# Ordering a bank's matrix products by width, and an earlier transpose of attention keys, in a ten-stage float32 network on Trainium2

## The chip, the cores and the metric

The kernel is one program on one core of a Trainium2 chip. The metric is the device time in microseconds of one execution; lower is better. Before the change it is 2365.12 us, the median of three runs. Engines are named as in the profile: PE (TensorE, matrix products), PEld (TensorE's loads of the stationary operand), DVE (VectorE), ACT (ScalarE), POOL (GpSimd) and SP (SyncE, which issues the DMAs).

## What is computed

Two blocks of two layers each, on 256 tokens of width 1024, in float32. The first has mixers (spatial gating with latent attention, and retention) and gated feed-forwards; the second puts in each layer a feed-forward, a hybrid of three attention branches, and a feed-forward. Cut to the two parts that the change touches:

```python
def swiglu(h, w_gate, w_up, w_down):
    return (jax.nn.silu(h @ w_gate) * (h @ w_up)) @ w_down

def swa_sink_attention(q, k, v, sinks):
    ...
    s = jnp.einsum('bnqhgd,bnkhd->bnhgqk', q, kb).astype(jnp.float32) * (D_C ** -0.5)
    s = s - slopes[:, :, None, None] * jnp.abs(dist).astype(jnp.float32)
    ...
    p = jax.nn.softmax(jnp.concatenate([s, sink], axis=-1), axis=-1)[..., :-1].astype(v.dtype)
    o = jnp.einsum('bnhgqk,bnkhd->bnqhgd', p, vb)

def hybrid_mixer(x, w_in, b_in, ...):
    proj = x @ w_in + b_in
    (qa, ka, va, beta_raw, a_raw, za, qb, kb, vb, qc, kc, vc) = jnp.split(proj, split_at, axis=-1)
    o_a = gated_deltanet(qa, ka, va, beta_raw, a_raw, za, ...)
    o_b = chunk_relpos_attention(qb, kb, vb, rel_bias)
    o_c = swa_sink_attention(qc, kc, vc, sinks)
    gates = jax.nn.sigmoid(x @ w_gate + b_gate).reshape(b, t, N_BRANCH, d)
    merged = (gates[:, :, 0] * (o_a @ w_br_a) + gates[:, :, 1] * (o_b @ w_br_b)
              + gates[:, :, 2] * (o_c @ w_br_c))
    return merged @ w_out
```

## The kernel before

**Stages.** Ten in a row: the even mixer, a feed-forward, the odd mixer, a feed-forward, then for each of two layers a feed-forward (32 column tiles of 128), a hybrid and a feed-forward. The 256 tokens are two blocks of 128. Activations stay in SBUF; the weights, 415.95 MB in all, are streamed once.

**Accuracy and weights.** Each float32 operand is split into a high and a low part of the type fp32r, and a product is three: high by high, high by low, low by high. `prep` (L137) brings a unit of weights, up to 128 x 2048, in two halves: a DMA on SP's queue into `raw` (L148, five buffers), a cast on ACT to `hi` (L149, four buffers) and a subtraction on DVE to `lo` (L150, four buffers). Up to four units are prepared ahead; `pump` and `more` issue them as units are used up.

**A bank of products.** `x_tile` (L350) makes 128 output columns for all 256 tokens in one PSUM bank of 512 float32 columns. The weights are the stationary operand. `x2[:, k]` holds the activations' high part beside their low part, 512 columns, and `xT[0][:, k]` the high part alone, 256 columns. For each of the eight slices k of the width, the weights' high part `u[0]` multiplies all 512 columns into the whole bank, and the weights' low part `u[1]` multiplies the 256 columns into its second half. A pair below is one such product of 512 and one of 256. `fold` (L360) then adds the halves: a copy on ACT (L263) and an addition on DVE (L241). `mm` (L230 in the trace) issues a product, `tr` (L238) a transpose, which is a product with the identity `ident`.

`apair` (L332) uses two banks for a unit (projections of the even mixer, and the hybrid's convolution inputs, queries, keys and gates); the feed-forward's `chunk` (L614) uses four, two of the gate and two of the up weights, and after it come the down products `emit_down` (L641), 512 columns each with activations as the stationary operand. PSUM's eight banks are four called acc and four called work. In a feed-forward acc holds the down projection's sums and the chunks use work; in a hybrid layer `x_tile` takes acc, and the attention tasks take work.

**A hybrid layer.** `bulk` (L1100) is a generator that issues the projections one after the other and announces events: "kvc" after the opening, in which keys and values of the grouped attention, the deltanet's beta and decay inputs and its gate za are projected; "qkv" after six `apair` of the convolution's inputs; "qc" after two for the grouped attention's queries; "qkvb" after those of the other attention. After each piece of `bulk` the tasks are stepped once: `tasks_cb` (the grouped attention `task_c`, L1203, then `task_b`) and `task_a` (the deltanet). So tasks fill in between projections. In `task_c` the keys of the two token blocks are transposed into a work bank, copied to `kcT` and multiplied by the queries; the alibi table is added (L253), `softmax` (L678) follows with exponentials on ACT, `p_T` (L702) transposes the weights p, ACT copies them out of PSUM, and PE multiplies them by the values. `task_a` transposes the deltanet's keys, values and queries to tokens, squares them on ACT, sums on DVE (L1323), takes the reciprocal root on POOL (L274) and multiplies on DVE.

**Order.** Each engine works off its own list in order. The framework's scheduler makes the lists from the program's order, the dependences and the buffers, so an edit in one place can move instructions of another task in a list.

Of the kernel before, what the change touches and what calls it, by code (L numbers as in the profile page):

```python
# [117 lines left out]
class Net:  # L118
# [231 lines left out]
    def x_tile(self, u, j):  # L350


        ps = self.acc() if self.gacc else self.work()
        c = slice(128 * j, 128 * j + 128)
        for k in range(8):
            self.mm(ps, u[0][:, k, c], self.x2[:, k], k == 0, False)
            self.mm(ps[:, 256:512], u[1][:, k, c], self.xT[0][:, k], False, k == 7)
        return ps

# [709 lines left out]
    def hyb(self, l, nxt):  # L1069
# [4 lines left out]
        events = set()  # L1074
# [8 lines left out]
        kvc = [None] * 2  # L1083
# [117 lines left out]
                    self.pump()  # L1201

        def task_c():  # L1203
            while "qc" not in events:
                yield "wait"
            kcT = self.tile(256)
            ps = self.work()
            for b in range(2):
                self.tr(ps[:, 128 * b:128 * b + 128], kvc[b][:, 0:128])
            self.cp(kcT, ps[:, 0:256])  # L1210
            ali = self.table("alibi", 384)
            yield
            qcT = late["qcT"]
            for b in range(2):
                nk = b + 1
                if b == 0:
                    oT[2] = self.pair(4)
                for half in range(2):
                    pr = slice(64 * half, 64 * half + 64)
                    s = self.tile(4, 128 * nk)  # L1220
                    for j in range(nk):
                        per = 4 // nk
                        bank = self.work()
                        for i in range(per):
                            h = per * j + i
                            c = slice(128 * nk * i, 128 * nk * i + 128 * nk)
                            self.mm(bank[:, c], qcT[pr, h, 128 * b:128 * b + 128], kcT[pr, 0:128 * nk])
                        for i in range(per):
                            h = per * j + i
                            c = slice(128 * nk * i, 128 * nk * i + 128 * nk)  # L1230
                            self.stt(s[:, h], ali[:, 128 * b:128 * b + 128 * nk], -float(2.0 ** -(4 * half + h + 1)), bank[:, c], ALU.mult, ALU.add)
                    p = self.softmax(s, 4, 128 * nk, 1.0, sinks[:, 4 * half:4 * half + 4])
                    yield
                    yield
                    pT = self.p_T(p, 4, nk)
                    yield
                    po = self.work()
                    pq = pT.rearrange("p (k e) n q -> p k e n q", e=2)
                    for e in range(2):
                        for kb in range(nk):  # L1240
                            self.mm(po[64 * e:64 * e + 64, 0:256].rearrange("p (k q) -> p k q", k=2), kvc[kb][:, 128 + 64 * half:192 + 64 * half],
                                    pq[:, :, e, kb], kb == 0, kb == nk - 1)
                    d = [t[:, 2 * half:2 * half + 2, 128 * b:128 * b + 128] for t in oT[2]]
                    self.split(d[0], d[1], po[:, 0:256].rearrange("p (k q) -> p k q", k=2))
                    yield
            events.add("o2")
# [266 lines left out]
        def tasks_cb():  # L1513
            yield from task_c()
            yield from task_b()
# [158 lines left out]
```

## Time and profile before

| | before |
|---|---|
| median of three runs | 2365.12 us (2364.11 to 2366.49) |
| the profiled execution | 2366.65 us, its span 2364.6 us |
| mean granted TensorE clock | 0.993 |
| PE busy | 2328.1 us, 98% of the span |
| DVE, ACT, POOL busy | 64%, 52%, 4% |
| chain that ended last | PE 96%, DVE 1%, POOL 1% |
| DMA | 419.14 MB, mean 177 GB/s |

Busy times are sums over instructions of one engine, from one profiled execution; the span leaves out some two microseconds of the time. A matmul's own duration in a row overlaps its neighbours', since matmuls are pipelined: the distance from one start to the next tells what one takes from the engine. The chain is followed backwards from the last instruction; an engine with nearly all of it sets the end. In the rows, a word in brackets is the idle time before an instruction and what ended it.

### The profile page before, as it was taken

What the parts mean: (1) busy time and instruction counts of PE and PEld (TensorE: products, weight loads), DVE (VectorE), ACT (ScalarE), POOL (GpSimd) and SP (SyncE); (2) the same over time, 40 slices, a digit from 0 to 9 for tenths busy, and PEclk for the clock granted to TensorE, in tenths of its full rate; (3) what the DMA queues carried; (4) which work ended last, traced back from release to release, by engine and by line L of the source; (5) the groups of instructions that cost most, each with busy time, mean ns of one, the idle gap of its engine ahead of it and who ended that gap; (6) DMA issues with size and microseconds to landing.
All of it is one profiled execution on the core that took longest, in us unless ns stands there. A gap on an engine that the chain in (4) does not pass through costs nothing.

```text
span 2364.6 us, 32735 instructions
## 1 busy us (share of the span) xinstructions
PE 2328.1 (98%) x12670; PEld 1991.7 (84%) x12670; DVE 1523.5 (64%) x2176; ACT 1232.0 (52%) x1942; POOL 94.2 (4%) x149
## 2 busy tenths in 40 slices
PE   8999999999999999999999999999999999999998
PEld 7788888888888888878998888888888789988887
DVE  6665576665565555887666555665567876765555
ACT  6655454454454544754545545455456644554543
POOL 4200000000000000000000000000000000000000
PEclk9999999999999999999999999999999999999999
DMA  7365555555556555543365555565555533565552
GB/s 238 131 210 192 189 193 174 186 186 187 189 181 208 191 186 175 188 143 119 100 205 201 191 187 187 178 210 185 191 173 195 168 103 100 185 209 186 193 185 92
DMA packets 120556, 419.14 MB, mean 177 GB/s; under 512 B 14408, under 2 KB 17224, under 8 KB 120400
## 3 DMA queue, kind: packets, MB, share of 16 engines
q1 hardware_dynamic: 120112, 416.53, 52.8%
q8 instruction: 99, 1.62, 0.3%
q14 instruction: 57, 0.47, 0.1%
q10 hardware_dynamic: 288, 0.52, 0.1%
HBM read 415.95 MB, written 1.05 MB: 176 GB/s over the span
## 4 chain that ended last, share of the span: by engine, by line
PE 96%; DVE 1%; POOL 1%; issue 0%; DMA 0%; ACT 0%; SPq 0%; POOLq 0%; DVEq 0%; ACTq 0%
PE work L230 51%; PE acc L230 42%; PE work L238 3%; DVE lo L150 1%; POOL c L273 0%; DMA raw<-in_w 0%; POOL c L274 0%; DVE s L241 0%; POOL c L853 0%; POOL c L852 0%; DVE s L253 0%; ACT s L260 0%; DVE c L1323 0%; ACT hi L149 0%; PE work L1437 0%
## 5 line engine op out<-in xcount | busy, mean ns | idle before, releaser
L150 DVE TENSOR_TENSOR lo<-raw,hi 128x1024 fp32r<-128x1024 f32 (+3 forms) x772 | 916.8, 1206 | 557.9 <-ACT hi L149 557.2
L149 ACT CAST hi<-raw 128x1024 fp32r<-128x1024 f32 (+3 forms) x772 | 786.0, 1038 | 547.0 <-PE work L230 210.9
L230 PE MATMUL work<-x,hi 128*128 128x512 f32 x2496 | 884.1, 398 | 0.0
L230 PE MATMUL work<-x,lo 128*128 128x256 f32 x2496 | 700.5, 281 | 0.0
L230 PEld LDWEIGHTS work<-x,hi 128*128 128x128 f32 x2496 | 468.9, 188 | 115.0
L230 PE MATMUL acc<-hi,s 128*128 128x512 f32 (+1 forms) x1736 | 555.9, 393 | 0.0
L230 PEld LDWEIGHTS work<-x,lo 128*128 128x128 f32 x2496 | 471.3, 189 | 2.7
L230 PEld LDWEIGHTS acc<-hi,s 128*128 128x128 f32 x1736 | 325.7, 188 | 70.9 <-DVE s L241 1.1
L230 PE MATMUL acc<-lo,s 128*128 128x512 f32 (+1 forms) x868 | 338.2, 390 | 0.0
L230 PE MATMUL acc<-x,hi 128*128 128x512 f32 x800 | 288.6, 403 | 0.0
L230 PE MATMUL acc<-x,lo 128*128 128x256 f32 x800 | 224.9, 281 | 0.0
L230 PE MATMUL work<-hi,x 128*128 128x512 f32 x640 | 205.4, 394 | 0.6 <-DVE x L241 0.5
L241 DVE TENSOR_TENSOR s<-s,s 128x512 f32<-128x512 f32 (+3 forms) x234 | 152.2, 658 | 64.9 <-ACT s L263 54.5
L263 ACT COPY s<-work 128x256 f32<-128x256 f32 (+3 forms) x380 | 151.2, 401 | 80.8 <-PE work L230 57.8
L230 PEld LDWEIGHTS acc<-lo,s 128*128 128x128 f32 x868 | 163.3, 188 | 31.3 <-issue 0.2
L241 DVE TENSOR_TENSOR s<-work,s 128x256 f32<-128x256 f32 (+5 forms) x382 | 165.0, 435 | 27.3 <-ACT s L263 14.3
L230 PEld LDWEIGHTS acc<-x,hi 128*128 128x128 f32 x800 | 151.2, 189 | 34.8
L263 ACT CAST s<-s 128x512 fp32r<-128x512 f32 (+2 forms) x90 | 54.5, 606 | 193.6 <-DVE s L241 193.6
L230 PEld LDWEIGHTS acc<-x,lo 128*128 128x128 f32 x800 | 152.0, 190 | 0.2
L230 PEld LDWEIGHTS work<-hi,x 128*128 128x128 f32 x640 | 119.9, 188 | 26.6 <-DVE x L241 1.8
L230 PE MATMUL work<-s,s 128*128 128x128 f32 (+8 forms) x884 | 125.2, 301 | 10.6 <-ACT s L263 9.9
L230 PEld LDWEIGHTS work<-s,s 128*128 128x128 f32 (+4 forms) x884 | 106.4, 185 | 26.5 <-ACT s L263 11.6
(108 smaller groups left out, 1597.7 us busy)
## 6 DMA issues: line engine op xcount, KB each, us to landing
raw<-in_w SPq DMA_DIRECT2D x748, 512.0 KB, 4.2
s<-in_rows SPq DMA_DIRECT2D x16, 512.0 KB, 6.7
raw<-in_w SPq DMA_DIRECT2D x12, 288.0 KB, 3.2
s<-in_rows SPq DMA_DIRECT2D x9, 256.0 KB, 5.6
raw<-in_w SPq DMA_DIRECT2D x4, 384.0 KB, 7.7
raw<-in_w SPq DMA_DIRECT2D x4, 256.0 KB, 4.4
s<-in_relb SPq DMA_DIRECT2D x2, 512.0 KB, 5.1
raw<-in_w SPq DMA_DIRECT2D x4, 240.0 KB, 2.5
```

Source lines behind the costliest of these rows:

```text
L149: self.nc.scalar.copy(hi[:, a:b], raw)
L150: self.nc.vector.tensor_tensor(out=lo[:, a:b], in0=raw, in1=hi[:, a:b].bitcast(F32), op=ALU.subtract)
L230: self.nc.tensor.matmul(out, lhsT=l, rhs=r, start=start, stop=stop)
L238: self.nc.tensor.transpose(out, src, self.ident)
L241: self.nc.vector.tensor_tensor(out=out, in0=a, in1=b, op=op)
L263: self.nc.scalar.copy(out, a)
```

## The change

Two edits. In `x_tile` the loop over k is split: all eight 512-column products with the weights' high part first, then all eight 256-column ones with the low part. In `task_c` the transposes of the keys and their copy are issued when "kvc" is there and one step has gone by, before the wait for "qc"; the alibi table's load stays behind that wait.

```diff
--- before.py
+++ after.py
@@ -354,6 +354,7 @@
         c = slice(128 * j, 128 * j + 128)
         for k in range(8):
             self.mm(ps, u[0][:, k, c], self.x2[:, k], k == 0, False)
+        for k in range(8):
             self.mm(ps[:, 256:512], u[1][:, k, c], self.xT[0][:, k], False, k == 7)
         return ps
 
@@ -1201,13 +1202,16 @@
                     self.pump()
 
         def task_c():
+            while "kvc" not in events:
+                yield "wait"
+            yield
+            kcT = self.tile(256)
+            ps = self.work()
+            for b in range(2):
+                self.tr(ps[:, 128 * b:128 * b + 128], kvc[b][:, 0:128])
+            self.cp(kcT, ps[:, 0:256])
             while "qc" not in events:
                 yield "wait"
-            kcT = self.tile(256)
-            ps = self.work()
-            for b in range(2):
-                self.tr(ps[:, 128 * b:128 * b + 128], kvc[b][:, 0:128])
-            self.cp(kcT, ps[:, 0:256])
             ali = self.table("alibi", 384)
             yield
             qcT = late["qcT"]
```

On PE in a feed-forward chunk, where `x_1160` is the activations and `hi`, `lo` are the weights' parts, the piece of the difference at the first bank reads:

```order
-L230 MATMUL work<-x_1160,hi 128x512
-L230 MATMUL work<-x_1160,lo 128x256
-L230 MATMUL work<-x_1160,hi 128x512
-L230 MATMUL work<-x_1160,lo 128x256
...
+L230 MATMUL work<-x_1160,hi 128x512 x8
+L230 MATMUL work<-x_1160,lo 128x256 x8
```

Sixteen products of changing width have become a run of eight and a run of eight; the sets are the same.

On PE in the first hybrid layer, around the grouped attention's first half (`acc_9202` a bank of projections, `work_9150` the transposes of the softmax's weights, `work_9183` their product with the values, `work_9188` and `work_9195` transposes of the deltanet's values), before:

```order
L230 MATMUL acc_9202<-x2_8142,lo_8900 128x256
L238 MATMUL work_9150<-ident_75,s2_9060 128x128 x4
L230 MATMUL acc_9202<-x2_8142,hi_8899 128x512
L230 MATMUL acc_9202<-x2_8142,lo_8900 128x256
L230 MATMUL work_9183<-s2_9149,s1_8330 64x256 x2
L238 MATMUL work_9188<-ident_75,s4_8642 128x128 x4
L238 MATMUL work_9195<-ident_75,s4_8642 128x128 x4
```

and now:

```order
L230 MATMUL acc_9202<-x2_8142,hi_8904 128x512 x3
L238 MATMUL work_9150<-ident_75,s2_9060 128x128 x4
L230 MATMUL acc_9202<-x2_8142,hi_8904 128x512 x5
L230 MATMUL acc_9202<-x2_8142,lo_8905 128x256 x8
L230 MATMUL work_9183<-s2_9149,s1_8330 64x256 x2
L238 MATMUL work_9188<-ident_75,s4_8647 128x128 x4
L238 MATMUL work_9195<-ident_75,s4_8647 128x128 x4
```

The transposes of the weights stood behind seven of the bank's eight pairs and stand behind three of its 512s; thirteen of the bank's products, not two, lie between them and the product with the values.

On ACT at the same place (`raw` and `hi_9156`, `hi_9272` weight units, `s2_9046` the scores, `work_9072` and `work_9112` transposed keys of the deltanet), before:

```order
L260 ACTIVATE s4_8960<-s2_9037,colt_80 128x256 x2
L149 CAST hi_9156<-raw_9158 128x1024
L260 ACT_TABLE_LOAD
L260 ACTIVATE s2_9060,c_9061<-s2_9046,c_9056 128x128 x4
L260 ACTIVATE c_9066<-c_9066 128x4
L260 ACTIVATE s2_9077<-work_9072 128x512
L149 CAST hi_9156<-raw_9162 128x1024
L149 CAST hi_9272<-raw_9274 128x1024
L260 ACTIVATE s2_9117<-work_9112 128x512
```

and now:

```order
L260 ACTIVATE s4_8965<-s2_9037,colt_80 128x256 x2
L260 ACT_TABLE_LOAD
L260 ACTIVATE s2_9060,c_9061<-s2_9046,c_9056 128x128 x4
L260 ACTIVATE c_9066<-c_9066 128x4
L260 ACTIVATE s2_9077<-work_9072 128x512
L149 CAST hi_9156<-raw_9158 128x1024
L149 CAST hi_9156<-raw_9162 128x1024
L260 ACTIVATE s2_9117<-work_9112 128x512
L149 CAST hi_9272<-raw_9274 128x1024
```

The first cast of unit 9156 stood ahead of the table load and the exponentials and stands behind the square of `work_9072`; the first cast of unit 9272 stood ahead of the square of `work_9112` and stands behind it.

On DVE there, before:

```order
L1323 TENSOR_REDUCE c_9078<-s2_9077 128x4
L150 TENSOR_TENSOR lo_9157<-raw_9162,hi_9156 128x1024
L241 TENSOR_TENSOR s2_9083<-work_9072,c_9078 128x512
L150 TENSOR_TENSOR lo_9273<-raw_9274,hi_9272 128x1024
L1323 TENSOR_REDUCE c_9118<-s2_9117 128x4
L150 TENSOR_TENSOR lo_9273<-raw_9278,hi_9272 128x1024
L241 TENSOR_TENSOR s2_9123<-work_9112,c_9118 128x512
```

and now:

```order
L1327 TENSOR_REDUCE c_9078<-s2_9077 128x4
L150 TENSOR_TENSOR lo_9157<-raw_9158,hi_9156 128x1024
L241 TENSOR_TENSOR s2_9083<-work_9072,c_9078 128x512
L1327 TENSOR_REDUCE c_9118<-s2_9117 128x4
L150 TENSOR_TENSOR lo_9157<-raw_9162,hi_9156 128x1024
L241 TENSOR_TENSOR s2_9123<-work_9112,c_9118 128x512
```

The reduction of the second square stood behind a subtraction of unit 9273 and follows the multiplication at once.

## Rows read from the trace of the kernel before

**Rows 1.** Page of before, busy time of each engine.
```profile
PE 2328.1 (98%) x12670; PEld 1991.7 (84%) x12670; DVE 1523.5 (64%) x2176; ACT 1232.0 (52%) x1942; POOL 94.2 (4%) x149
```

**Rows 2.** Page, costliest groups: busy us, mean ns of one; idle before.
```profile
L230 PE MATMUL work<-x,hi 128*128 128x512 f32 x2496 | 884.1, 398 | 0.0
...
L230 PEld LDWEIGHTS work<-x,lo 128*128 128x128 f32 x2496 | 471.3, 189 | 2.7
...
L230 PE MATMUL acc<-x,hi 128*128 128x512 f32 x800 | 288.6, 403 | 0.0
```

**Rows 3.** Timeline of PE, 32 pairs of a chunk: start us, us, instruction, [idle before].
```profile
610.79 0.39 PE L230 MATMUL work<-x,hi 128*128 128x512 f32 x1
...
622.08 0.40 PE L230 MATMUL acc<-hi,s 128*128 128x512 f32 x1
```

**Rows 4.** Timeline of PE, 512-column products of the down projection, same view.
```profile
607.84 0.62 PE L230 MATMUL acc<-hi,s 128*128 128x512 f32 x2
...
610.56 0.39 PE L230 MATMUL acc<-hi,s 128*128 128x512 f32 x1
```

**Rows 5.** Timeline of PE, a run of 256 columns and the 512 behind.
```profile
1220.37 0.40 PE L230 MATMUL acc<-s,hi 128*128 128x256 f32 x2
...
1226.49 0.40 PE L230 MATMUL acc<-hi,s 128*128 128x512 f32 x1
...
1228.33 0.62 PE L230 MATMUL acc<-hi,s 128*128 128x512 f32 x2
```

**Rows 6.** Timeline of PE, grouped attention in both hybrid layers.
```profile
1020.93 0.38 PE L238 MATMUL work<-ident,s 128*128 128x128 f32 x2
...
1041.71 0.65 PE L230 MATMUL work<-s,s 128*64 128x256 f32 x4 [3.53 <-ACT s L263]
...
1045.55 1.09 PE L238 MATMUL work<-ident,s 128*128 128x128 f32 x4 [2.14 <-DVE s L241]
...
1882.93 1.09 PE L238 MATMUL work<-ident,s 128*128 128x128 f32 x4 [1.67 <-DVE s L241]
```

**Rows 7.** Windows: us, busy (x) of PE, PEld, DVE, ACT, POOL, PEclk, DMA share, GB/s.
```profile
1042.30:1052.50 10.20, 8.06 (x33) 6.84 (x32) 6.83 (x18) 3.93 (x14) 2.11 (x2) 0.50 0.43 130
76.30:83.10 6.80, 5.88 (x15) 4.64 (x16) 6.20 (x16) 4.74 (x11) 1.21 (x2) 0.50 0.26 80
66.00:73.00 7.00, 6.35 (x42) 5.74 (x43) 4.71 (x10) 4.62 (x8) 5.97 (x10) 1.00 0.22 75
```

**Rows 8.** Timeline of PE, 264 columns right after 512 columns, a hybrid layer's opening.
```profile
954.91 0.28 PE L230 MATMUL acc<-hi,x 128*128 128x264 f32 x1
...
955.88 0.40 PE L230 MATMUL acc<-hi,x 128*128 128x264 f32 x2
```

**Rows 9.** Timeline of ACT ahead of the first hybrid layer's wait.
```profile
1031.82 1.05 ACT L149 CAST hi<-raw 128x1024 fp32r<-128x1024 f32 x1 [0.57 <-ACT s L260]
1032.88 1.28 ACT L260 ACT_TABLE_LOAD   x1
1034.18 0.40 ACT L260 ACTIVATE s<-s,c 128x128 f32<-128x128 f32 x1
```

**Rows 10.** Timeline of DVE, same place.
```profile
1032.57 0.16 DVE L241 TENSOR_TENSOR c<-c 128x4 f32<-128x4 f32 x1
...
1040.59 1.22 DVE L150 TENSOR_TENSOR lo<-raw,hi 128x1024 fp32r<-128x1024 f32 x1
...
1044.71 0.69 DVE L241 TENSOR_TENSOR s<-work,c 128x512 f32<-128x512 f32 x1 [1.18 <-POOL c L274]
```

**Rows 11.** Timeline of SP's queue, same layer.
```profile
1016.99 17.49 SPq L148 DMA_DIRECT2D raw<-in_w  x8
```

**Rows 12.** Timeline of PE, the first stage's two longer waits.
```profile
66.65 0.64 PE L238 MATMUL work<-ident,s 128*96 128x128 f32 x4 [1.18 <-POOL s L854]
...
76.55 1.23 PE L230 MATMUL work<-s,s 128*128 128x128 f32 x4 [2.85 <-ACT s L263]
```

**Rows 13.** Timeline of PEld, weight loads in a run of 256-column products.
```profile
1127.47 0.31 PEld L230 LDWEIGHTS acc<-s,hi 128*128 128x128 f32 x2
...
1128.55 0.31 PEld L230 LDWEIGHTS acc<-s,hi 128*128 128x128 f32 x2
```

More of the change, by code (lines that the diff above doesn't have):

```diff
@@ L1203, in task_c @@
         def task_c():
-            while "qc" not in events:
+            while "kvc" not in events:
                 yield "wait"
+            yield
             kcT = self.tile(256)
@@ L1210, in task_c @@
             self.cp(kcT, ps[:, 0:256])
+            while "qc" not in events:
+                yield "wait"
             ali = self.table("alibi", 384)
```

## The prediction

> **What bounds the kernel now.** I read the busy times first. TensorE (PE) works 2328.1 of 2364.6 us of span [rows 1], so a microsecond counts if TensorE's own instructions get shorter or one of its few waits does. The costliest groups come next: the products that the change reorders are 2496 in work banks and 800 in acc banks, each with a 256-column partner [rows 2]. At eight pairs to a bank that is 3296 / 8 = 412 banks. The durations there (398 and 403 ns) overlap with the neighbours, so no price comes out of them. What a product costs is the distance between starts, from the timeline. In a feed-forward chunk 32 pairs go from 610.79 to 622.08 [rows 3]: 11.29 us, 352.8 ns a pair, **2.822 us a bank**. Products of one width in a row run closer than their shares of that pair: 512 after 512 go from 607.84 to 610.56, 12 in 2.72 us, 226.7 ns each [rows 4], and 256 after 256 take 6.12 us for 51, 120.0 ns each [rows 5]. The sum of the two is 346.7, not 352.8: changing the width costs about 6 ns a pair. Last I looked for TensorE's long waits. Past the opening there are few, and the largest are in the two hybrid layers: 3.53 us before the grouped attention's product of weights and values, then 2.14 us before a transpose in the first layer and 1.67 in the second [rows 6], with the clock at 0.50, the 1.2 GHz level, for 10.2 us from there [rows 7].
>
> **The change, part by part.** *Grouping.* No product is added or removed; a bank keeps its 8 + 8, and the last is still the one that closes it. The width now changes twice a bank instead of sixteen times. What a short run of eight costs has two rows near it. Eight 512-column products right after a run of 256 take 1.84 us, from 1226.49 to 1228.33 [rows 5] (230 ns each: the first ones are slower than the steady 226.7). Eight products of 264 columns right after 512-column ones take 0.97 us, from 954.91 to 955.88 [rows 8]; eight columns less each at 2.4 GHz, the level of a granted clock of 1.00, is 8 x 8 / 2.4 = 27 ns, so 0.943. The new bank is 1.842 + 0.943 = 2.785 us, the gain 0.037 us, times 412 = **15.2 us**. The low end takes the steady 120.0 ns for the 256 (bank 2.802, gain 8.2), the high end the steady 226.7 for the 512 (bank 1.814 + 0.960 = 2.774, gain 20). I take the middle: it comes from the rows nearest to a run of eight behind the other width. A gain of nothing is a rival below.
>
> Against this stands a rule. In these rows a product's price hangs on the one before it (352.8 against 346.7). The Trainium skill, "TensorE: Matmul & The Clock Gate", section "Back-to-back issue gap", gives an isolated gap of columns / 2.4 plus 2.5 ns, in any order: by that a bank is 8 x (215.8 + 109.2) = 2.600 us before and after, and the grouping gains nothing. The trace differs: it shows 2.822.
>
> *What the grouping moves on the other engines.* The low part of a weight unit is wanted eight products later, its high part is free about eight 256-column products (0.96 us) sooner: both ease the casts. As the high buffer is free sooner, its next casts slip ahead of the fold of the bank on ScalarE, and the subtractions ahead of the fold's add on VectorE. Two casts of 1.05 [rows 9], two subtractions of 1.22 [rows 10] and the fold itself are under 6 us; the chunk has four work banks, so a bank is wanted again after three others, 8.4 us. That covers it: nothing. Were the cover gone, the rest would be a TensorE wait at every fourth bank.
>
> *The keys' transposes.* Two transposes, a work bank and a copy go from the point where the queries are ready to the opening of the layer. They are 0.38 us for both as shown [rows 6], about 0.25 in spacing, on TensorE at either place. No engine waits by the generator's wait itself; it decides only where the instructions are issued. The alibi table's DMA (128 x 384, 0.2 MB) falls behind one weight transfer on SP's queue, the first of the eight that were issued from 1016.99 [rows 11]; each of the two is 1.5 to 4 us at the 130 GB/s of a neighbouring stretch [rows 7] (0.2 and 0.5 MB), so it lands by about 1023, and the scores need it shortly ahead of the softmax's last step at 1032.57 [rows 10]. The weight transfer gets ahead of it, which hurts none. Nothing, with several microseconds of cover.
>
> *The hybrid layers' stall.* Both parts reorder the queues here. Before, one cast (1031.82, 1.05 us) stands ahead of the table load (1.28) and so of the softmax's exponentials, which start at 1034.18 [rows 9], though their inputs are there at 1032.57 + 0.16 = 1032.73 [rows 10]. Now the cast comes behind them: 1.4 us. On VectorE a subtraction (1040.59, 1.22 us with its overlap, some 1.1 in spacing) stands ahead of the reduction that the late transpose hangs on by way of POOL and the multiplication at 1044.71 [rows 10]; now the reduction is first: 1.1. The transpose at 1045.55 would be 2.5 us earlier. Of this, the banks between 1020.93 and 1041.71 (some 6 outside the wait) have 0.22 in the grouping's sum already, and 0.25 are the two transposes that only change place: 2.0 a layer, **4.0 us** for both. Ends: 2.5 a layer if nothing is counted twice; a loss of 1.05 if one cast now stands ahead of the copy that the attention waits for. I take the 2.0, since the moves stand in the order. Next late is that copy: between the transposes of the softmax weights and the product that waits, TensorE now has five 512s and eight 256s (2.1 us) instead of one pair (0.35), but they come out of the work ahead, and by estimate some 2.5 us of wait stays there, then 1.2 before the transpose.
>
> **Sum.** 15.2 + 4.0 = 19.2. The profiled execution took 2366.65 us, 1.53 over the median 2365.12; 2366.65 - 19.2 - 1.53 = 2345.9, so **2346.0**.
>
> **The rivals.**
> A, the sum as it stands, clock falling in both layers as before. Its own range is 2340 (20 and 5.0) to 2357 (8.2 and nothing): for it speak [rows 5, 8].
> C, the clock no longer falls in the hybrid layers. The rest of that stretch, 1045.55 to 1052.50, is 6.95 us at the lower level, and 3.5 us come back in each: 2342.4 for one, 2338.9 for both. What the rows say of shorter waits: one wait of 2.85 us, in the first stage, is followed by 0.50, and one of 1.18 by 1.00 [rows 7, 12]. The remaining 2.5 is nearer to 2.85, so C is the less likely.
> B, a product's price does not depend on its neighbours after all, and the 6 ns are lost somewhere else (an operand's place, say): only the 4.0 remain, 2361.1. Against it: the same widths show both prices in one chunk [rows 3, 4]. This is also what the skill's rule above gives; its level disagrees with the trace, so it adds little to the chance.
> D, slower: eight 256-column products in a row leave too little time to load their weights. A load's row is 188 to 189 ns [rows 2]; now a 512-column product stands between two 256s and hides it. If a load had to run by itself, the bank would be 1.84 + 8 x 0.189 = 3.35 us, 0.53 more, 218 in all: 2579. It decides from 122 ns a product ((2.822 - 1.842) / 8). Against it: in a 256-column run nine loads start within 1.08 us, 120 ns apart, though each is shown as 0.19 [rows 13]; those load activations, not weights, the one thing that differs.
>
> **How the numbers follow.** A 0.57, C 0.23, B 0.10, D 0.05, the rest (a partial gain, a new wait that eats some of it) 0.05. The forecast is A's. The range takes A's slow end and C's time for both layers with 2 us for the bank's spread: 2337 to 2357, holding A and C, 0.80 or a little more. About 0.2%, 4.7 us, can be told from no change. Faster: A, C and most of the rest, 0.85. Same: B, 0.10. Slower: D, 0.05.
>
> **What would show it.** In the changed profile a feed-forward bank takes 2.78 to 2.79 us from first start to first start, eight 512s about 1.84 and eight 256s about 0.94. 2.82 would be B; 256s at 188 ns would be D; a bank of 2.80 or 2.774 moves the sum by its 412-fold. In each hybrid layer the product after the softmax still waits for its copy, about 2.5 us, and the late transpose about 1.2 us instead of 2.14; a granted clock of 1.00 behind them is C. New TensorE waits for ScalarE or VectorE at every fourth bank of a chunk would mean that the fold's delay was not covered, and would make the prediction wrong from the side that I priced at nothing.

## The result and the profile after

The change takes 2341.69 us, the median of four runs (2340.47 to 2342.30), against 2365.80 for the kernel before in the same measurement: a ratio of 0.9898 with a 95% interval of 0.9881 to 0.9916. That is 24.1 us less; the forecast was 2346.0, and the range of 2337 to 2357 holds it. The profiled execution took 2340.47 us, its span 2338.4, at a mean granted clock of 0.996 (0.993 before).

The page of the change, busy times and the two groups of [rows 2]:

```profile
PE 2308.1 (99%) x12670; PEld 1992.8 (85%) x12670; DVE 1536.9 (66%) x2176; ACT 1230.9 (53%) x1942; POOL 94.5 (4%) x149
...
L230 PE MATMUL work<-x,hi 128*128 128x512 f32 x2496 | 624.1, 392 | 0.0
...
L230 PE MATMUL acc<-x,hi 128*128 128x512 f32 x800 | 205.5, 399 | 0.0
```

PE's busy sum is 20.0 us smaller than in [rows 1], with as many instructions. The busy sum of the 512-column products fell from 884.1 to 624.1; that is no saving of 260 us, since a group counts the time of overlapping products once, and in a run they overlap one another. Only distances tell.

The timeline of PE in a feed-forward chunk of the change, as in [rows 3]:

```profile
622.99 1.98 PE L230 MATMUL work<-x,hi 128*128 128x512 f32 x8
624.80 1.12 PE L230 MATMUL work<-x,lo 128*128 128x256 f32 x8
625.76 2.00 PE L230 MATMUL work<-x,hi 128*128 128x512 f32 x8
627.60 1.12 PE L230 MATMUL work<-x,lo 128*128 128x256 f32 x8
628.55 2.00 PE L230 MATMUL work<-x,hi 128*128 128x512 f32 x8
...
634.13 0.40 PE L230 MATMUL acc<-hi,s 128*128 128x512 f32 x1
```

Four banks go from 622.99 to 634.13: 11.14 us, 2.785 a bank, as the prediction's sum of [rows 5, 8] had it. In a bank in the middle, eight 512s take 625.76 to 627.60, 1.84 us, and eight 256s 0.95.

The timeline of PE in the two hybrid layers of the change, at the places of [rows 6]:

```profile
1032.42 0.65 PE L230 MATMUL work<-s,s 128*64 128x256 f32 x4 [2.21 <-ACT s L263]
...
1034.69 1.08 PE L238 MATMUL work<-ident,s 128*128 128x128 f32 x4 [0.82 <-DVE s L241]
```

```profile
1860.20 0.65 PE L230 MATMUL work<-s,s 128*64 128x256 f32 x4 [2.20 <-ACT s L263]
...
1861.76 0.63 PE L238 MATMUL work<-ident,s 128*128 128x128 f32 x4 [0.31 <-DVE s L241]
```

The wait before the product with the values fell from 3.53 to 2.2 us in both layers, and the one before the late transpose from 2.14 and 1.67 to 0.82 and 0.31 (in the second layer 0.33 us more stands before the transposes behind it). For the second layer, [rows 6, 7] have only the late transpose; its other wait before the change, and the window from there, are:

```profile
1879.10 1.12 PE L230 MATMUL work<-s,s 128*64 128x256 f32 x4 [3.53 <-ACT s L263]
```

```profile
1878.60:1888.80 10.20, 8.04 (x32) 6.16 (x33) 7.92 (x19) 3.29 (x9) 2.11 (x2) 0.50 0.46 140
```

The windows of the change behind those waits (columns as in [rows 7]):

```profile
1033.50:1040.50 7.00, 6.18 (x26) 5.11 (x25) 6.64 (x15) 2.62 (x7) 0.32 (x1) 0.53 0.45 153
1860.00:1870.00 10.00, 9.16 (x51) 6.64 (x52) 7.69 (x18) 4.21 (x15) 0.89 (x1) 1.00 0.49 148
```

In the first layer the clock still falls to 0.50, for about 6.8 us instead of 10.2. In the second it stays at 1.00 in this execution: this is rival C in one of two layers.

### The profile page after: what moved, and what is told of

The parts are those of the page before. It is cut to its first block, busy times and chain, and to the rows that moved or that the text cites. A ratio compares the mean times of both kernels' runs of the same rounds, so it can differ in the third digit from the quotient of the medians.

```text
span 2338.4 us, 32717 instructions
## 1 busy us (share of the span) xinstructions
PE 2308.1 (99%) x12670; PEld 1992.8 (85%) x12670; DVE 1536.9 (66%) x2176; ACT 1230.9 (53%) x1942; POOL 94.5 (4%) x149
## 4 chain that ended last, share of the span: by engine, by line
PE 54%; DVE 1%; POOL 1%; issue 0%; ACT 0%; POOLq 0%; DVEq 0%; ACTq 0%
PE work L230 27%; PE acc L230 26%; PE work L238 2%; DVE lo L150 0%; POOL c L273 0%; POOL c L274 0%; DVE s L241 0%; DVE s L253 0%; DVE c L1327 0%; ACT s L260 0%; PE work L1441 0%; POOL c L549 0%; DVE s L540 0%; DVE x L241 0%; POOLq L1674 0%
## 5 line engine op out<-in xcount | busy, mean ns | idle before, releaser
L150 DVE TENSOR_TENSOR lo<-raw,hi 128x1024 fp32r<-128x1024 f32 (+3 forms) x772 | 904.0, 1207 | 452.3 <-ACT hi L149 449.4
L149 ACT CAST hi<-raw 128x1024 fp32r<-128x1024 f32 (+3 forms) x772 | 766.6, 1036 | 413.8 <-PE work L230 141.7
L230 PE MATMUL work<-x,hi 128*128 128x512 f32 x2496 | 624.1, 392 | 0.0
L230 PEld LDWEIGHTS work<-x,hi 128*128 128x128 f32 x2496 | 453.5, 189 | 83.8
L230 PEld LDWEIGHTS work<-x,lo 128*128 128x128 f32 x2496 | 340.6, 191 | 24.3
L230 PE MATMUL work<-x,lo 128*128 128x256 f32 x2496 | 348.3, 283 | 0.0
L230 PE MATMUL acc<-x,hi 128*128 128x512 f32 x800 | 205.5, 399 | 0.0
L230 PEld LDWEIGHTS acc<-x,hi 128*128 128x128 f32 x800 | 144.3, 189 | 26.9 <-issue 1.0
L260 ACT ACTIVATE s<-s 128x512 f32<-128x512 f32 (+1 forms) x120 | 83.5, 696 | 157.1 <-DVE s L241 138.6
L230 PE MATMUL work<-lo,x 128*128 128x512 f32 x320 | 124.9, 390 | 0.0
```

The source lines that it names most:

```text
L149: self.nc.scalar.copy(hi[:, a:b], raw)
L150: self.nc.vector.tensor_tensor(out=lo[:, a:b], in0=raw, in1=hi[:, a:b].bitcast(F32), op=ALU.subtract)
L230: self.nc.tensor.matmul(out, lhsT=l, rhs=r, start=start, stop=stop)
L260: self.nc.scalar.activation(out=out, in_=a, func=fn, scale=scale, bias=bias, **k)
```

## Experiments

**One part alone, twice.** First the grouping without the move:

```diff
 for k in range(8):
     self.mm(ps, u[0][:, k, c], self.x2[:, k], k == 0, False)
-    self.mm(ps[:, 256:512], u[1][:, k, c], self.xT[0][:, k], False, k == 7)
+for k in range(8):
+    self.mm(ps[:, 256:512], u[1][:, k, c], self.xT[0][:, k], False, k == 7)
```

> Only the loop over k is split; the keys' transposes stay where the queries are ready. Its order on ScalarE and VectorE around the hybrid layers' wait is that of before: the cast stands ahead of the table load again. Theory (grouping is worth 0.037 us a bank, and the hybrid layers gain only when both edits are made): 15 us less than before, some 2350.5, and both hybrid layers still show a granted clock of 0.50 behind a wait of about 3 us. Rival 1 (the keys' move is idle, grouping alone does everything): the time of the whole change, about 2342. Rival 2 (most of the gain is the hybrid layers'): over 2355.

Measured: 2349.61 us (2348.58 to 2351.25) against 2366.72, ratio 0.9928 (0.9915 to 0.9942), 17.1 us less. In its first hybrid layer PE's timeline still shows two long waits, 5.3 us together where [rows 6] had 5.67, and a new one of 0.66 ahead of them. Over the whole span TensorE is idle as long as before: 2349.2 less 2313.0 us busy is 36.2, against 36.5. The windows behind the long waits show the lower level in both layers:

```profile
1030.84 0.63 PE L238 MATMUL work<-ident,s 128*128 128x128 f32 x4 [0.66 <-DVE s L241]
...
1035.35 0.65 PE L230 MATMUL work<-s,s 128*64 128x256 f32 x4 [2.70 <-ACT s L263]
...
1039.19 1.09 PE L238 MATMUL work<-ident,s 128*128 128x128 f32 x4 [2.60 <-DVE s L241]
```

```profile
1036.00:1046.50 10.50, 7.90 (x31) 6.58 (x31) 6.77 (x18) 4.29 (x17) 2.11 (x2) 0.53 0.41 126
1866.00:1876.80 10.80, 8.74 (x34) 6.67 (x35) 7.81 (x19) 3.90 (x13) 2.10 (x2) 0.53 0.43 137
```

Then the move without the grouping, with `x_tile` as before and `task_c` as in the change.

> Only the keys' transposes are moved; the pairs of 512 and 256 columns alternate as before. The order around the hybrid layers' wait is that of before. Theory (no gain without the grouping): within 2 us of before, 2364 to 2368, same waits of 3.5 us and the same two stretches at 0.50. Rival (the keys' move by itself makes the hybrid layers faster): 2356 to 2362.

Measured: 2366.06 us against 2366.72, ratio 0.9999 (0.9990 to 1.0008): no change, with waits of 3.53 and 1.67 us in the first layer and both stretches at 0.50. So 17 of the 24 us are the grouping's, none is the move's alone, and about 7 come only when both are made (the grouping alone and the change, 2349.61 and 2341.69, are 7.9 apart). ScalarE's timelines, the grouping alone first, then the move alone:

```profile
1025.47 1.03 ACT L149 CAST hi<-raw 128x1024 fp32r<-128x1024 f32 x1
1026.52 1.28 ACT L260 ACT_TABLE_LOAD   x1
```

```profile
1030.36 1.05 ACT L149 CAST hi<-raw 128x1024 fp32r<-128x1024 f32 x1 [0.23 <-ACT s L260]
1031.42 1.28 ACT L260 ACT_TABLE_LOAD   x1
```

Neither edit by itself takes the cast from its place ahead of the table load, and both together do. Other instructions change places with it (the reduction on VectorE, for one), and no run moved the cast alone, so that it is this cast is argued, not shown.

**How long the runs must be.** In groups of four:

```diff
-for k in range(8):
-    self.mm(ps, u[0][:, k, c], self.x2[:, k], k == 0, False)
-for k in range(8):
-    self.mm(ps[:, 256:512], u[1][:, k, c], self.xT[0][:, k], False, k == 7)
+for g in range(0, 8, 4):
+    for k in range(g, g + 4):
+        self.mm(ps, u[0][:, k, c], self.x2[:, k], k == 0, False)
+    for k in range(g, g + 4):
+        self.mm(ps[:, 256:512], u[1][:, k, c], self.xT[0][:, k], False, k == 7)
```

> Both edits, but a bank runs four 512s, four 256s, four 512s, four 256s: the width changes 4 times a bank instead of 16 (before) or 2 (the change). On ScalarE around the hybrid wait the order is that of before, so 0 to 1 us is to be had there. Theory A (every return to 512 columns costs about 27 ns over the steady price, spread over the first five products, and the first 256 behind a 512 gives 6 back; in an alternation each pair pays 6): half a bank is 931 + 473 ns, a bank 2.808, gain 0.014 x 412 = 6 us, 2359 to 2360. Theory B (each change of width costs the same, 0.037 / 14 us): gain 0.032 x 412 = 13 us, 2352 to 2353.

Measured: 2356.78 us against 2366.72, ratio 0.9958 (0.9946 to 0.9971), 9.9 us less, between the two theories. PE's timeline has the bank's own price:

```profile
610.04 1.09 PE L230 MATMUL work<-x,hi 128*128 128x512 f32 x4
...
611.45 1.09 PE L230 MATMUL work<-x,hi 128*128 128x512 f32 x4
...
612.85 1.09 PE L230 MATMUL work<-x,hi 128*128 128x512 f32 x4
...
615.66 1.09 PE L230 MATMUL work<-x,hi 128*128 128x512 f32 x4
```

Two banks take 610.04 to 615.66, 2.81 us each, where theory A said 2.808 and B 2.790; over all 312 work banks, from start to next start, it is 2.803. A is the nearer for the price. The median gained more than A's 6 us. Part of the rest lies behind the banks: the down products that follow a chunk take 464.0 us by their distances instead of 465.4. What made up the remainder was not singled out; the wait before the product with the values is 3.18 instead of 3.53.

Then two banks of a weight unit together in the chunks (`x_part` makes one kind of product for both banks):

```diff
-for j in range(2):
-    self.fold(p, j, self.x_tile(u, j))
+pj = [self.work() for j in range(2)]
+for i in range(2):
+    self.x_part(u, pj, i)
+for j in range(2):
+    self.fold(p, j, pj[j])
```

> The whole change, and in the feed-forward chunks the two banks of a weight unit go together: sixteen 512s, then sixteen 256s. The hybrid layers' order is the change's. 156 such pairs of banks. Theory A (a return to 512 costs some 21 ns net however long the runs): 3.3 us less than the change, about 2338.5. Theory B (each change of width costs 0.037 / 14 us): 0.8 us less, about 2341. Rival (the folds, now both at the end of two banks, come late for the silu and the next bank): slower than the change, with TensorE waits for ScalarE or VectorE in the chunks.

Measured: 2339.95 us (2339.45 to 2342.62), ratio 0.9890 (0.9876 to 0.9903), 1.7 us under the change. From the start of each of these products to the next start, summed over the trace, the 312 work banks took 880.6 us before, 870.4 in the change and 867.6 here: 2.9 us, near A's 3.3 and far from B's 0.8. In the total most of it is within the spread. And all four banks of a chunk together, the two units taken first and the folds last:

> The whole change, and in the chunks all four banks go together: thirty-two 512s, then thirty-two 256s. Theory A (each return to 512 that is saved gives 18 ns, as sixteen and sixteen gave 0.037 us a chunk for two): three returns fewer than the change in 78 chunks, 0.055 us a chunk, 4.3 us less than the change, 2337 to 2338, a chunk of some 11.09 us. Rival (folds of four banks end late and the gate's silu and the next use of the work banks wait for them): TensorE waits appear ahead of the products that use the chunk's result or the next chunk's banks, and the time is over 2342.

Measured: 2339.73 us (2337.13 to 2342.22), ratio 0.9889 (0.9874 to 0.9903): no slower, so the folds are covered even there, and in the total not told apart from two banks. The work banks took 865.9 us, 4.5 under the change, where A says 4.3. PE's timeline:

```profile
608.01 7.42 PE L230 MATMUL work<-x,hi 128*128 128x512 f32 x32
615.27 4.00 PE L230 MATMUL work<-x,lo 128*128 128x256 f32 x32
```

Thirty-two 512s take 7.26 us, 226.9 ns each, the steady price; a chunk is 7.26 + 32 x 0.120 = 11.10.

**Is it the width?** The kernel before with each 512-column product cut in two:

```diff
-self.mm(ps, u[0][:, k, c], self.x2[:, k], k == 0, False)
+self.mm(ps[:, 0:256], u[0][:, k, c], self.xT[0][:, k], k == 0, False)
+self.mm(ps[:, 256:512], u[0][:, k, c], self.xT[1][:, k], False, False)
 self.mm(ps[:, 256:512], u[1][:, k, c], self.xT[0][:, k], False, k == 7)
```

> The kernel before with every 512-column product cut into two of 256 columns with the same weights, still alternating high and low weights in every slice: 24 products of one width a bank, the same sums. Theory (the price of an alternation is that of changing the width): all products stand 120 ns apart, 2.88 us a bank, though the weights' tile still alternates. Rival (the price is that of changing between the weights' two tiles): 6 ns more per slice, 2.93 us a bank. Either way slower than before by 24 to 44 us.

PE's timeline of it:

```profile
599.88 0.28 PE L230 MATMUL work<-x,lo 128*128 128x256 f32 x1
600.00 0.40 PE L230 MATMUL work<-x,hi 128*128 128x256 f32 x2
600.24 0.28 PE L230 MATMUL work<-x,lo 128*128 128x256 f32 x1
```

A slice (low, high, high) takes 0.36 us, 120 ns a product, though the weights' tile alternates as before: the price of the alternation is that of the width, not of changing between the weights' two tiles (nor between the halves of the bank, which alternate too). The whole took 2376.14 us in its one run, 10 more than before where 412 x 0.0575 = 23.7 was to be paid. By the same sum over starts the banks' products take 21.5 us more (1198.1 against 1176.6), and all else some 11.5 less (1158.3 against 1169.8). Much of that is shorter waits: with more work for TensorE ahead of them, the hybrid layers have 2.10 us left before the product with the values, nothing before the transpose, and one stretch at 0.50.

**The waits that stayed.** One more piece of projections between the transposes of the softmax's weights and the product with the values:

```diff
 pT = self.p_T(p, 4, nk)
 yield
+yield
```

> The whole change, and the grouped attention lets one more piece of the projections pass between the transposes of the softmax's weights and their product with the values, so that TensorE has a bank and a product more ahead of the product that waits for ScalarE's copy. Theory (the waits of 2.2 and 0.8 us cost themselves and, in the first layer, 3.3 us more by the stretch at 0.50): the wait shrinks to under 0.5, no stretch at 0.50 stays in either hybrid layer, 5 to 8 us less than the change, 2334 to 2337. Rival (the wait only moves on, to the deltanet's transposes behind POOL and VectorE, and the clock falls there): within 2 us of the change's 2341.7.

Measured: 2343.09 us (2342.13 to 2345.99), ratio 0.9905 (0.9890 to 0.9920): nothing gained. The rival's time was right, its place only in part; PE's timeline in the first layer:

```profile
1033.89 0.63 PE L238 MATMUL work<-ident,s 128*128 128x128 f32 x4 [1.16 <-DVE s L241]
...
1037.82 0.47 PE L230 MATMUL acc<-x,hi 128*128 128x512 f32 x1 [2.59 <-DVE s L241]
```

The wait before the product with the values is gone. The deltanet's transposes wait 1.16 us, as the rival said, and a projection waits 2.59 us for its bank, which VectorE has not folded yet; both layers still have a stretch at 0.50. So the late copy was not all that held TensorE up. The same kernel with two banks at a time in the chunks:

> The edits of the two kernels that should each gain, together: two banks of a unit at a time in the chunks, and one more piece of projections ahead of the grouped attention's product with the values. Theory (they touch different stages and add): 2.9 us from the chunks and 5 to 8 from the hybrid layers, 2331 to 2334. Rival (one of the two gains nothing): 2336 to 2341.

Measured: 2340.92 us, ratio 0.9894 (0.9877 to 0.9910): the step gains nothing here either.

What holds VectorE is seen in the change's own queues, DVE first, then POOL:

```profile
1027.26 0.68 DVE L1327 TENSOR_REDUCE c<-s 128x4 f32<-128x512 f32 x1
1027.85 1.22 DVE L150 TENSOR_TENSOR lo<-raw,hi 128x1024 fp32r<-128x1024 f32 x1
1030.26 0.69 DVE L241 TENSOR_TENSOR s<-work,c 128x512 f32<-128x512 f32 x1 [1.19 <-POOL c L274]
1030.87 0.67 DVE L1327 TENSOR_REDUCE c<-s 128x4 f32<-128x512 f32 x1
1031.46 1.22 DVE L150 TENSOR_TENSOR lo<-raw,hi 128x1024 fp32r<-128x1024 f32 x1
1033.86 0.69 DVE L241 TENSOR_TENSOR s<-work,c 128x512 f32<-128x512 f32 x1 [1.18 <-POOL c L274]
1034.46 0.74 DVE L241 TENSOR_TENSOR s<-acc,s 128x256 f32<-128x256 f32 x2
```

```profile
1028.02 1.10 POOL L273 TENSOR_SCALAR c<-c 128x4 f32<-128x4 f32 x1 [19.05 <-DVE c L1327]
1029.20 1.02 POOL L274 TENSOR_TENSOR c<-c,nh 128x4 f32<-128x4 f32 x1
1031.63 1.10 POOL L273 TENSOR_SCALAR c<-c 128x4 f32<-128x4 f32 x1 [1.40 <-DVE c L1327]
```

VectorE waits for POOL's root 1.19 and 1.18 us, with the folds behind it in its queue, and POOL's first instruction ends, 1.10 us after its start, when VectorE's subtraction (1027.85 to 1029.07, 1031.46 to 1032.68) does, to within 0.05 us. The next kernel takes both lengths before the first multiplication:

```diff
 for b in range(2):
-    ps = tokens(kT, b)
-    rk = lengths(ps)
-    kt[b] = self.tile(512)
-    self.mul(by_head(kt[b]), by_head(ps), self.bc(rk, 128))
-    yield
-yield
+    ks[b] = tokens(kT, b)
+    rk[b] = lengths(ks[b])
+    if b == 0:
+        yield
+scaled(0)
+yield
+scaled(1)
+yield
```

where `scaled(b)` makes the tile and multiplies.

> The whole change, and the deltanet's two key lengths are taken before the first of the two multiplications that use them, so POOL's two reciprocal roots no longer stand one after the other with VectorE waiting 1.2 us for each; on ScalarE the copy that the product with the values waits for then stands behind two casts instead of four. Theory (the waits in the hybrid layers are this chain of queues, and the stretch at 0.50 follows them): the wait of 2.2 falls to under 1, the one before the transpose vanishes, no stretch at 0.50 in at least one layer: 3 to 8 us less than the change, 2334 to 2339. Rival (the wait moves on to another queue, as in the kernel with one step more): within 2 us of the change.

Measured: **2332.18 us** (2331.21 to 2333.02) against 2364.73, ratio 0.9861 (0.9844 to 0.9877). The unaltered change ran beside it:

> The whole change, unaltered, beside the three kernels below. Theory: 2340 to 2343 as before, the wait of about 2.2 us before the grouped attention's product with the values in both hybrid layers. Whether the clock falls in the second hybrid layer, which it did not in the first profile of the change, would tell whether that belongs to the kernel or to the single execution.

Measured: 2341.67 us (2340.29 to 2341.89), ratio 0.9898 (0.9884 to 0.9913). So the two roots side by side are worth 9.5 us, more than the 3 to 8 expected. By the profiled executions somewhat over half of it is TensorE's idle time, which falls from 30.1 us (2339.8 less 2309.7) to 24.5 (2329.1 less 2304.6); the other 5.1 of the 10.7 us between the spans are half of the 6.8 and 3.4 us at 0.50 that the unaltered change has in the two layers and this kernel has not. POOL, and the windows over both hybrid layers' places, with the roots side by side:

```profile
1027.30 0.19 POOL L273 TENSOR_SCALAR c<-c 128x4 f32<-128x4 f32 x1 [19.05 <-DVE c L1327]
1027.57 1.02 POOL L274 TENSOR_TENSOR c<-c,nh 128x4 f32<-128x4 f32 x1
1028.68 0.19 POOL L273 TENSOR_SCALAR c<-c 128x4 f32<-128x4 f32 x1
```

```profile
1024.00:1040.00 16.00, 15.79 (x92) 12.51 (x91) 12.69 (x26) 10.85 (x30) 2.42 (x4) 1.00 0.42 133
1850.00:1866.00 16.00, 16.00 (x98) 12.90 (x97) 13.90 (x29) 10.34 (x28) 2.27 (x5) 1.00 0.47 147
```

PE is busy all but 0.21 us of 32, at a clock of 1.00. And the windows of the second layer in the unaltered change's second profile:

```profile
1861.00:1864.70 3.70, 3.66 (x15) 2.35 (x16) 2.58 (x5) 1.52 (x5) 1.01 (x1) 0.54 0.48 142
```

There the clock fell in the second layer, which it had not in the first profile, behind the same wait of 2.20 us: whether it falls there belongs to the execution, not to the kernel. The two spans, 2339.8 with the 3.4 us at 0.50 and 2338.4 without, are 1.4 apart, near half of that stretch.

Then the copy of the first softmax weights on VectorE as well, and with that two banks at a time in the chunks:

```diff
-pT = self.p_T(p, 4, nk)
+pT = self.p_T(p, 4, nk, 4 - 4 * b)
...
-    if i % 8 == 0:
+    if i % 8 == o:
         self.cp(flat[:, 128 * i:128 * i + 512], ps)
```

> As the kernel with the roots side by side, and the copy of the first softmax weights goes to VectorE, which is idle there, instead of ScalarE behind its casts. Theory: no wait over 0.5 us is left before the product with the values, both hybrid layers at a granted clock of 1.00: 6 to 10 us less than the change, 2332 to 2336. Rival (VectorE's own queue holds the copy up as long): the time of the kernel with the roots side by side, within 1.5 us.

> The last kernel's edits and two banks of a unit at a time in the chunks. Theory (different stages, so they add): 2.9 us less than the last kernel, 2329 to 2333. Rival (the chunks' gain is within the spread and the hybrid layers' gains do not come): over 2337.

Measured: 2333.16 us (2332.17 to 2334.52), ratio 0.9864 (0.9849 to 0.9879), no better than the roots alone: 0.59 us of wait came back in the first layer, now for VectorE's copy. The time lies in the ranges of both; the wait and the missing gain speak for the rival. With the two banks 2330.53 us (2329.30 to 2330.79), ratio 0.9851 (0.9837 to 0.9866), 2.6 under that: the fastest kernel here, 34 us under the one before and 11 under the change.

## Why the prediction was right, point by point

*The grouping, 15.2 us.* Right in mechanism and in total, with parts that differ from the sum's. The four banks shown above take the 2.785 us of the sum, but the mean of the 312 work banks is 2.790, against 2.822 before: a gain of 10.2 us, 0.033 each instead of 0.037. The term that was sized a little too low is the 256s': eight of them take 0.952 us (114 ns, 119, then 120 each), where 0.943 was worked out from [rows 8]. The acc banks, by the mean distances of the grouping alone where no task's product stands between (349.0 ns a pair instead of 351.8), gain some 2.2 us. To make up for it, the gain does not end with the bank, which the prediction did not see: the 512-column down products that follow a chunk take 462.9 us instead of 465.4, 2.5 less. Together that is some 15.0; that the errors nearly cancel is luck. The median of the grouping alone fell by 17.1, with an interval of 14 to 20, but its profiled execution by 15.4 (2351.25 against 2366.65), with TensorE idle as long as before: in its first hybrid layer the wait before the product with the values is 0.83 shorter, the late transpose's 0.46 longer, and one of 0.66 is new. The groups of four and of sixteen and the kernel of one width agree that the price is one of width and is paid at the return to 512 columns.

*The moves on the other engines, nothing.* Right: PE has no new waits in the chunks, not even with the folds behind four banks.

*The keys' transposes, nothing.* Right alone (ratio 0.9999).

*The hybrid layers, 4.0 us.* The term that was mis-sized: some 7 us come there (24.1 less 17.1). The step for the waits held. They sum to 3.03 us in the first layer instead of 5.67, 2.6 less, where the prediction left 2.5 and 1.2 and so took 2.0 off. What failed is the step "clock falling in both layers as before": the stretch in the first layer was 6.8 us instead of 10.2, and the second had none in one profile and about 3.4 in another. The price of rival C, half of the stretch, fits the two profiles of the change (1.4 us for 3.4); that it would come in part and by execution was not foreseen. The time for C in one layer, 2342.4, is the nearest of the rivals' to the measured 2341.7: the forecast was A's, and what was measured is nearer to C in part.

*What was late next.* Right in name (ScalarE's copy, then the transpose), and 2.2 us where 2.5 was said. But the copy was only where the wait showed. The chain behind it goes through VectorE's wait for POOL, which [rows 10] already had in brackets (1.18 us for POOL), and it was worth more than the whole term.

*Rivals.* D is out: 256-column products with weights as the stationary operand run at 120 ns. B is out: it left the grouping no gain, and the grouping alone gained 17.1; the kernel of one width rules out the change of tile as the place of the loss. The formula of the Trainium skill ("TensorE: Matmul & The Clock Gate", "Back-to-back issue gap") has no term for the neighbour, and the traces differ from it: the first five 512s behind a run of 256s measure 229 to 236 ns, 512 after 512 measure 226.7, and its isolated gap is 215.8.

## What to carry to other kernels

Where TensorE sets the time, read products' distances by what stands before them, and put products of one width in runs: here the runs of eight brought most of it (11.16 us a chunk on average instead of 11.29), and a run of thirty-two 0.06 us more per chunk. Where a wait moves when it is covered, follow the queue of the engine that releases it back to an instruction that idles in front of others; here it paid to start two small operations on POOL before the first result was used. And when two edits reorder shared queues, try each alone before crediting either.

## What was not expected of the hardware

The length of the wait ahead does not by itself settle whether the clock falls. Behind the same 2.20 us before the product with the values, the second hybrid layer had no stretch at 0.50 in one profile of the change, about 3.4 us in another, and over 6 in the kernel with four banks in a chunk (there 0.65 us before the transpose came on top), whose window reads:

```profile
1862.00:1868.50 6.50, 6.50 (x26) 5.46 (x25) 6.43 (x15) 2.62 (x7) 0.00 (x0) 0.50 0.35 118
```

What tips it was not tried, and stays open.

POOL's small multiply-and-add took 1.10 us while VectorE subtracted two SBUF tiles, ending with it, and 0.19 where VectorE was reducing or reading PSUM. The Trainium skill has this in "SBUF — State Buffer", section "Who interferes with whom": a VectorE instruction with two SBUF inputs and a GpSimd instruction that reads SBUF share a port, and the later one waits out the other. The traces agree, at 0.9 us an instruction (spans on POOL are rough); how much of the 9.5 us is this, and how much the shorter queue ahead of ScalarE's copy (two casts instead of four), was not separated.

The return from 256 to 512 columns costs about 27 ns spread over five products. In the change's bank from 614.73 the distances of the first two are 233 and 237 ns by start times, in the steady run 226.7. Behind an alternation it lasts longer: of the down products that follow a chunk, the first ten together take some 57 ns over the steady price before the change, and 27 with the grouping, where it is over after five (means over 68 chunks in each trace). Why it takes five products, or ten, to settle was not tried.
